# A hybrid attention and state-space decoder layer on Trainium2: score and value matmuls in alternating halves of the array, and the first score behind the middle of the next projection slab

## The chip, the cores and the metric

The kernel runs on one core of a Trainium2 chip. The time is the device time of one execution, in microseconds (us), as a median of runs. One further execution was taken by the hardware profiler; all lines of the profile below are from it. TensorE is PE in the profile (PEld are its weight loads), VectorE is DVE, ScalarE is ACT, GpSimd is POOL, SyncE is SP.

## The reference

One step of a one-layer hybrid decoder: a prompt of 2048 tokens, and 8 sequences with 4 new tokens each (the decode part). One input projection feeds a state-space (Mamba-2) head group and a sliding-window attention head group, then come an output projection, a normalised residual and a feed-forward part. The change lies in the attention of the prompt, which in the reference is

```python
def swa_prompt(q, k, v, sinks):            # window 128: a block and the block before it
    qb = q.astype(jnp.float32).reshape(b, nb, WINDOW, N_KV, Q_PER_KV, HEAD_DIM)   # 16 blocks, 2 x 4 heads of 64
    ...
    s = jnp.einsum('bnqgrd,bnkgd->bngrqk', qb, kk) * (HEAD_DIM ** -0.5)
    s = jnp.where(mask[None, :, None, None], s, -jnp.inf)
    p = sink_softmax(s, sinks.astype(jnp.float32).reshape(N_KV, Q_PER_KV)[:, :, None, None])
    o = jnp.einsum('bngrqk,bnkgd->bnqgrd', p, vv)
    return o.reshape(b, t, ATT_WIDTH).astype(q.dtype)
```

with `q` and `k` turned by a rotary embedding on the first quarter of each head.

## The kernel before

The kernel goes through the tokens in sweeps. Sweep 1 handles the 16 prompt tiles of 128 tokens (and, as one more tile, the decode tokens): it normalises and transposes a tile, projects it to 776 columns (step sizes, q, k, v) and does the attention. Sweep 2 does the state-space part, then follow the output projection and the feed-forward part, which together take most of the time. Tiles are counted from one in this document.

In sweep 1 the work of a tile is cut into steps, and a loop over places calls, at each place, the steps of several tiles: the first slab of 388 columns of tile t (`st_slab(t,0)`), the transposes of the probabilities of tile t-2 (`st_PT`), the scores of tile t-1 (`st_score`), the second slab of tile t, a step of the modulation vector (line 258) or of the decode attention, the values of tile t-2 (`st_PV`), and the transposes of q and k of tile t (`st_qkT`). The calls only set a first order. A scheduler then orders the instructions of TensorE, VectorE, ScalarE and GpSimd by its own model of their times, so that a step's instructions stand among those of others. [...]

To keep precision every operand of the large products is split into a high and a low part, and a product is three matmuls (`mm3`, lines 166 to 168): high with high, high with low, low with high. A slab is 8 x 3 of them, 128 x 128 by 388 columns.

The scores of a tile are 24 matmuls with 64 rows of contraction, by 256 columns (its own block and the one before). The 8 heads lie so that even heads (`par` 0) are in partitions 0 to 63 and odd heads (`par` 1) in partitions 64 to 127, that is, in the lower and the upper half of the array's rows. For each key head g and each `par` six matmuls go into one PSUM bank, and the bank is then copied into `S`, by ScalarE (L434) and by a predicated copy on VectorE (L435), which frees it. After it come the softmax (L384 to L394), and in `st_PT` the transposes (L450) and their copies (`PT` on ScalarE, `PC` on VectorE, L453). The values are four float32 matmuls (L462): two terms, each for g 0 and 1, where g chooses the half of the array's columns. PSUM has three banks for scores and values (`sc`), three for projections (`mm`) and two for transposes (`tr`), each kind used in turn.

Other names: `rt` are the products of the rotary embedding (L374, L375), `qh`, `ql`, `kTh` and `kTl` the split transposes of q and k (L407, L411), `Wx` and `pg` split weights, `xproj` the projection of the convolution's inputs for sweep 2 (`mm<-hT,Wx` and `mm<-hT,pg`), of which the first block's eight run at the end of sweep 1, `dkw` the decays, and `zproj` the first projection of sweep 2 (`mm<-pg,hT`).

Of the kernel before, what the change touches and what calls it, by code (L numbers as in the profile page):

```python
# [119 lines left out]
def body(tc, I, O):  # L120
    nc = tc.nc
    V, S, G, PE, D = nc.vector, nc.scalar, nc.gpsimd, nc.tensor, nc.sync
# [8 lines left out]
    def mm_tile():  # L131
        return ps.tile([128, 512], F32, tag="mm", name="mm", bufs=3)
# [4 lines left out]
    def sc_tile():  # L137
        return ps.tile([128, 512], F32, tag="sc", name="sc", bufs=3)
# [11 lines left out]
    def mm_dec(tmp, w, hs, wt):  # L150
        acc = mm_tile()
        for k in range(8):
            for l in range(2):
                PE.matmul(acc[:2 * ND, :w], lhsT=hs(k), rhs=wt(k, l), start=k + l == 0, stop=k + l == 8)
        S.activation(tmp[:2 * ND, :w], acc[:2 * ND, :w], AF.Copy)
        return tmp

    def sum2(out, tmp, w):
        PE.matmul(out[:ND, :w], lhsT=idt[:2 * ND, 192:224], rhs=tmp[:2 * ND, :w], start=True, stop=True)

    def split(hi, lo, src, eng=None):
        S.activation(hi, src, AF.Copy)  # L162
        (eng or V).tensor_tensor(lo, src, hi.bitcast(F32), ALU.subtract)  # L163

    def mm3(out, ahi, alo, bhi, blo, first=True, last=True):
        PE.matmul(out, lhsT=ahi, rhs=bhi, start=first, stop=False)  # L166
        PE.matmul(out, lhsT=ahi, rhs=blo, start=False, stop=False)  # L167
        PE.matmul(out, lhsT=alo, rhs=bhi, start=False, stop=last)  # L168

    def rstd_of(p, var, P, n=1, scale=1.0):  # L170
        v = p.tile([128, n], F32, tag="ve%d" % n, name="ve", bufs=2)
# [15 lines left out]
    def ptok(t):  # L187
        return 128 if t < NTILE else ND
# [11 lines left out]
    def page(i):  # L200
        return pw.tile([128, 1024], F32R, tag=f"pg{i}", name=f"pg{i}")
# [30 lines left out]
    start = ExitStack()  # L232
# [49 lines left out]
    W1h = [page(k)[:, 0:776] for k in range(8)]  # L282
    W1l = [page(8 + k)[:, 0:776] for k in range(8)]
# [15 lines left out]
    kTh = p1.tile([128, 2, 3, 128], F32R, name="kTh")  # L299
    kTl = p1.tile([128, 2, 3, 128], F32R, name="kTl")  # L300
    tl = {}
# [45 lines left out]
    def st_slab(t, n):  # L347
        P = ptok(t)
        hh = tl["hT", t]
        if n == 0:  # L350
            tl["qkv", t] = p1.tile([128, 648], F32, tag="qkv", name="qkv", bufs=2)
            tl["v", t] = p1.tile([128, 128], F32, tag="v", name="v", bufs=5)
        qkv = tl["qkv", t]
        mm = tl.pop(("sm", t, n)) if t < 3 else mm_tile()
        sl = slice(388 * n, 388 * n + 388)
        if t == NTILE:
            tmp = mm_dec(p1.tile([128, 512], F32, tag="ao", name="tmp", bufs=2), 388, lambda k: hh[:, 0, k, :2 * ND],
                         lambda k, l: (W1l if l else W1h)[k][:, sl])
            sum2(mm, tmp, 388)
        elif t > 2:  # L360
            for k in range(8):
                mm3(mm[:P, :388], hh[:, 0, k, :P], hh[:, 1, k, :P], W1h[k][:, sl], W1l[k][:, sl], k == 0, k == 7)
        if n == 0:
            S.activation(qkv[:P, sl], mm[:P, :388], AF.Copy)
            V.tensor_copy(dt_all[:P, t, :], qkv[:P, 0:8])
            return
        S.activation(qkv[:P, 388:648], mm[:P, 0:260], AF.Copy)
        S.activation(tl["v", t][:P], mm[:P, 260:388], AF.Copy)
        qk = qkv[:P, 8:648].rearrange("p (h d) -> p h d", h=10)
        cos = cc(C_COS + 16 * t, 16)[:P].unsqueeze(1).to_broadcast([P, 10, 16])  # L370
        sin = cc(C_SIN + 16 * t, 16)[:P].unsqueeze(1).to_broadcast([P, 10, 16])
        t1 = p1.tile([128, 10, 16], F32, tag="rt1", name="rt1", bufs=1)
        t2 = p1.tile([128, 10, 16], F32, tag="rt2", name="rt2", bufs=1)
        V.tensor_tensor(t1[:P], qk[:, :, 0:16], cos, ALU.mult)  # L374
        V.tensor_tensor(t2[:P], qk[:, :, 0:16], sin, ALU.mult)  # L375
        V.tensor_tensor(qk[:, :, 0:8], t1[:P, :, 0:8], t2[:P, :, 8:16], ALU.add)
        V.tensor_tensor(qk[:, :, 8:16], t1[:P, :, 8:16], t2[:P, :, 0:8], ALU.add)

    def softmax(p, Sx, P, nh, nk, sink):
        mx = p.tile([128, 8], F32, tag="mx", name="mx", bufs=2)  # L380
        nm = p.tile([128, 8], F32, tag="nm", name="nm", bufs=2)
        su = p.tile([128, 8], F32, tag="su", name="su", bufs=2)
        ex = p.tile([128, 8], F32, tag="ex", name="ex", bufs=2)
        V.tensor_reduce(mx[:P, :nh], Sx, AX.X, ALU.max)  # L384
        V.scalar_tensor_tensor(mx[:P, :nh], mx[:P, :nh], 0.125, sink, ALU.mult, ALU.max)
        V.tensor_scalar(nm[:P, :nh], mx[:P, :nh], -1.0, None, ALU.mult)
        V.tensor_tensor(ex[:P, :nh], sink, mx[:P, :nh], ALU.subtract)
        S.activation(ex[:P, :nh], ex[:P, :nh], AF.Exp)
        for h in range(nh):
            S.activation(Sx[:, h, :], Sx[:, h, :], AF.Exp, bias=nm[:P, h:h + 1], scale=0.125,  # L390
                         accum_out=su[:P, h:h + 1])
        V.tensor_tensor(su[:P, :nh], su[:P, :nh], ex[:P, :nh], ALU.add)
        V.reciprocal(su[:P, :nh], su[:P, :nh])
        G.tensor_tensor(Sx, Sx, su[:P, :nh].unsqueeze(2).to_broadcast([P, nh, nk]), ALU.mult)  # L394
# [20 lines left out]
    def st_score(t):  # L415
        qh, ql = tl.pop(("q", t))
        if t == 0:
            slots, nk, ci = slice(0, 1), 1, 0
        else:
            slots, nk, ci = [(slice(0, 3, 2), 2, 0), (slice(0, 2), 2, 1), (slice(1, 3), 2, 1)][t % 3]  # L420
        ge = cc(C_GE, 128).bitcast(U32).unsqueeze(1).to_broadcast([128, 2, 128])
        Sx = p1.tile([128, 8, 128], F32, tag="S", name="S", bufs=2)
        if t == 0:
            V.memset(Sx, NEG)
        for g in range(2):
            for par in range(2):
                sc = sc_tile().rearrange("p (j s n) -> p j s n", j=2, s=2)
                rp = slice(64 * par, 64 * par + 64)
                for jj in range(2):
                    q2 = 2 * g + jj  # L430
                    mm3(sc[:, jj, 0:nk, :], qh[rp, q2, :], ql[rp, q2, :], kTh[rp, g, slots, :], kTl[rp, g, slots, :])
                hs = slice(4 * g + 2 * par, 4 * g + 2 * par + 2)
                if t > 0:
                    S.activation(Sx[:, hs, :], sc[:, :, 1 - ci, :], AF.Copy)  # L434
                V.copy_predicated(Sx[:, hs, :], ge, sc[:, :, ci, :])  # L435
        softmax(p1, Sx, 128, 8, 128, sm[:, 3, :])
        tl["S", t] = Sx
# [19 lines left out]
    def st_PV(t):  # L457
        terms = tl.pop(("PT", t))
        o = sc_tile()
        for i, (vv, pt) in enumerate(terms):  # L460
            for g in range(2):
                PE.matmul(o[64 * g:64 * g + 64, :], lhsT=vv[:, 64 * g:64 * g + 64], rhs=pt[:, g, :],  # L462
                          start=i == 0, stop=i == len(terms) - 1, tile_position=(0, 64 * g))
        ao = p1.tile([128, 4, 128], F32, tag="ao", name="ao", bufs=2)
        S.activation(ao.rearrange("p r n -> p (r n)"), o, AF.Copy)
        S.dma_start(out=att_d[t], in_=ao)
# [219 lines left out]
    n = len(seq)  # L686
# [66 lines left out]
    for i in range(n + 3):  # L753
        if i == 10:
            start.close()
        g = lambda j: seq[j] if 0 <= j < n else None
# [7 lines left out]
        if t is not None:  # L764
            st_slab(t, 0)
        if g(i - 2) is not None and g(i - 2) < NTILE:
            st_PT(g(i - 2))
        if g(i - 1) is not None and g(i - 1) < NTILE:
            st_score(g(i - 1))
        if t is not None:  # L770
            st_slab(t, 1)
        if i >= 1 and extras:
            extras.pop(0)()
        if g(i - 2) is not None and g(i - 2) < NTILE:
            st_PV(g(i - 2))
# [566 lines left out]
    def dec_steps():  # L1342
# [12 lines left out]
        for n in range(2):  # L1355
            sum2(pp[n], b[:, 512 * n:512 * n + 512], 512)
# [166 lines left out]
```

## Time and profile before

| | |
|---|---|
| median of 3 runs | 2485.43 us (2485.16 to 2487.25) |
| profiled execution, its own time | 2483.86 us |
| its span | 2482.0 us |
| TensorE busy | 2407.5 us, 97% of the span |
| VectorE, ScalarE, GpSimd busy | 1466.3, 764.0, 883.4 us |
| scores of sweep 1, first to last | 66.2 to 391.5 us |

The profile gives for each group of instructions its line, engine, operation, output and inputs by the program's names, shapes, count and busy time. In a timeline a row has start, duration, engine, line, names and the number of records; where an engine sat idle before the row, a bracket gives how long and what ended it. The recorded ends of matmuls are modelled, and successive matmuls overlap in the record. A row of a table by stretches gives for each engine the busy time in the stretch and the number of instructions, then the clock that TensorE was granted (1.00 is full) and the share of the DMA engines.

### The profile page before, as it was taken

Reading aid. Unit: us, or ns where it says so; the run is one execution under the profiler, and the core shown is the slowest. Engines: PE = TensorE matmul, PEld = TensorE weight load, DVE = VectorE, ACT = ScalarE, POOL = GpSimd, SP = SyncE. Lnnn points to the kernel's source line nnn. Section 1 sums busy time; section 2 is a strip of 40 time slices with the busy share of each in tenths; the row PEclk is TensorE's granted clock in tenths of the full one; section 3 lists DMA queues with packets and bytes.
Section 4 is the critical chain, followed back from the end, with each engine's and each line's share of the span. In section 5 each row is a group of like instructions: output and inputs, shape, how many; then the busy total and the mean of one; then the engine's idle time right before and its main releaser. Section 6 shows DMA issues by size and latency. Waiting matters only on the chain.

```text
span 2482.0 us, 32262 instructions
## 1 busy us (share of the span) xinstructions
PE 2407.5 (97%) x12695; PEld 2000.0 (81%) x12695; DVE 1466.3 (59%) x2549; ACT 764.0 (31%) x1546; POOL 883.4 (36%) x587
## 2 busy tenths in 40 slices
PE   7899999999999999899999999999999999999997
PEld 6567777987997888787888888887888888888885
DVE  6756665977788776845444344448744354354347
ACT  3544465432444545221211212112212212212221
POOL 4323430233233222642433424337422332332335
PEclk9999999999999999999999999999999999999998
DMA  8654242223315348221111211119210111111111
GB/s 317 255 186 163 89 157 84 73 67 120 98 62 190 128 161 285 90 66 56 59 43 43 64 43 54 49 37 267 74 52 34 43 60 34 43 60 35 43 47 70
DMA packets 116104, 242.11 MB, mean 98 GB/s; under 512 B 26080, under 2 KB 61360, under 8 KB 112800
## 3 DMA queue, kind: packets, MB, share of 16 engines
q1 hardware_dynamic: 111552, 230.07, 27.6%
q10 hardware_dynamic: 4400, 9.98, 1.0%
q8 instruction: 100, 1.64, 0.3%
q14 instruction: 52, 0.43, 0.1%
HBM read 185.66 MB, written 55.37 MB: 97 GB/s over the span
## 4 chain that ended last, share of the span: by engine, by line
PE 82%; DVE 10%; issue 3%; ACT 2%; POOL 2%; DMA 1%; POOLq 0%; DVEq 0%; SPq 0%; ACTq 0%
PE mm L166 12%; PE mm L168 12%; PE mm L167 12%; PE sc L166 11%; PE sc L167 11%; PE sc L168 11%; PE tr L166 2%; PE tr L168 2%; PE tr L167 2%; PE sc L462 1%; DVE xc L653 1%; PE mm L258 1%; DVE p L1230 1%; DVE csb L858 1%; PE tr L1275 1%
## 5 line engine op out<-in xcount | busy, mean ns | idle before, releaser
L163 POOL TENSOR_TENSOR wdl<-st,wdh 128x1024 fp32r<-128x1024 f32 x63 | 151.6, 2406 | 537.7 <-ACT wdh L162 537.6
L1260 DVE TENSOR_TENSOR r<-r 128x320 f32<-128x320 f32 (+1 forms) x160 | 146.4, 915 | 298.0 <-ACT u L1256 104.7
L1287 DVE TENSOR_TENSOR p<-mm,p 128x512 f32<-128x512 f32 x298 | 202.5, 687 | 175.2 <-PE mm L168 175.2
L162 ACT ACTIVATE wdh<-st 128x1024 fp32r<-128x1024 f32 x63 | 66.8, 1061 | 646.8 <-PE mm L168 263.3
L166 PE MATMUL sc<-H,wvh 128*128 128x352 f32 (+1 forms) x640 | 225.5, 352 | 5.5 <-ACT r L1254 5.5
L167 PE MATMUL sc<-H,wvh 128*128 128x352 f32 (+1 forms) x640 | 225.9, 353 | 0.0
L168 PE MATMUL sc<-H,wvl 128*128 128x352 f32 (+1 forms) x640 | 225.5, 352 | 0.0
L166 PE MATMUL sc<-H,wuh 128*128 128x352 f32 (+1 forms) x640 | 223.8, 350 | 0.0
L168 PE MATMUL sc<-H,wul 128*128 128x352 f32 (+1 forms) x640 | 223.1, 349 | 0.0
L167 PE MATMUL sc<-H,wuh 128*128 128x352 f32 (+1 forms) x640 | 222.8, 348 | 0.0
L1254 ACT ACTIVATE r<-sc 128x352 f32<-128x352 f32 (+1 forms) x160 | 81.5, 510 | 263.9 <-PE sc L168 225.9
L166 PEld LDWEIGHTS sc<-H,wvh 128*128 128x128 f32 x640 | 120.6, 188 | 18.2 <-ACT r L1254 5.9
L167 PEld LDWEIGHTS sc<-H,wvh 128*128 128x128 f32 x640 | 120.6, 188 | 12.3
L168 PEld LDWEIGHTS sc<-H,wvl 128*128 128x128 f32 x640 | 120.5, 188 | 12.1
L166 PEld LDWEIGHTS sc<-H,wuh 128*128 128x128 f32 x640 | 120.1, 188 | 11.1 <-ACT r L1254 0.8
L168 PEld LDWEIGHTS sc<-H,wul 128*128 128x128 f32 x640 | 120.4, 188 | 10.3
L167 PEld LDWEIGHTS sc<-H,wuh 128*128 128x128 f32 x640 | 120.3, 188 | 10.1
L174 POOL TENSOR_TENSOR rs<-ve,mhalf 128x1 f32<-128x1 f32 (+2 forms) x68 | 48.5, 714 | 207.5 <-DVE ve L173 182.7
L1137 DVE TENSOR_TENSOR st<-st,gf 128x1024 f32<-128x1024 f32 x64 | 86.6, 1353 | 50.6 <-POOL wdl L163 42.4
L1259 DVE TENSOR_TENSOR ud<-r 128x32 f32<-128x32 f32 x32 | 58.4, 1825 | 93.8 <-ACT r L1254 93.8
L1287 DVE TENSOR_TENSOR p<-tr,p 128x512 f32<-128x512 f32 x102 | 69.9, 687 | 73.8 <-PE tr L168 73.6
L1261 POOL TENSOR_TENSOR ulx<-r,x 128x512 fp32r<-128x512 f32 (+2 forms) x52 | 76.6, 1475 | 83.5 <-DVE r L1260 83.5
(485 smaller groups left out, 6608.9 us busy)
## 6 DMA issues: line engine op xcount, KB each, us to landing
st<-in_wd SPq DMA_DIRECT2D x64, 512.0 KB
st<-in_wu SPq DMA_DIRECT2D x63, 512.0 KB
wa<-in_w_ada SPq DMA_DIRECT2D x32, 512.0 KB
hT_d<-hb SPq DMA_DIRECT2D x16, 1024.0 KB
hT<-hT_d SPq DMA_DIRECT2D x16, 512.0 KB
hT<-hT_d SPq DMA_DIRECT2D x8, 1024.0 KB
csb<-cs_d SPq DMA_DIRECT2D x16, 512.0 KB
p<-xhat_d SPq DMA_DIRECT2D x16, 512.0 KB
```

Source lines behind the costliest of these rows:

```text
L162: S.activation(hi, src, AF.Copy)
L163: (eng or V).tensor_tensor(lo, src, hi.bitcast(F32), ALU.subtract)
L166: PE.matmul(out, lhsT=ahi, rhs=bhi, start=first, stop=False)
L167: PE.matmul(out, lhsT=ahi, rhs=blo, start=False, stop=False)
L168: PE.matmul(out, lhsT=alo, rhs=bhi, start=False, stop=last)
L174: G.tensor_tensor(r[:P], v[:P], mhalf[:P, 0:n], ALU.pow)
L1137: V.tensor_tensor(st, raw, scale, ALU.mult)
L1254: S.activation(r[:, :n], mm[:, :n], AF.Relu)
L1259: V.tensor_tensor(ud, r[:, w:n], r[:, w:n], ALU.mult)
L1260: V.tensor_tensor(r[:, :w], r[:, :w], r[:, :w], ALU.mult)
L1261: G.tensor_tensor(ul[:, o:o + w], r[:, :w], uh[:, o:o + w].bitcast(F32), ALU.subtract)
L1287: V.tensor_tensor(acc[t][:, sl], mm, acc[t][:, sl], ALU.add)
```

## The change

A helper `side_by_side` issues a list of matmuls and gives each an ordering after the one before it in the list. The ordering is one for the scheduler (`NoSync`): it fixes their order in TensorE's row and adds no semaphore. The scores of a key head use it with the two halves in turn (`par` 1, 0, 1, 0 ...) and both banks taken ahead of them; for g = 1 the second half's bank is now one of the projection banks. The first score of a tile is ordered behind the twelfth of the 24 matmuls of the next tile's first slab (`tl["mid"]`, from the fourth tile on). The four value matmuls get the same helper, with g 1, 0, 1, 0.

```diff
+    def side_by_side(calls, prev=None):
+        for fn in calls:
+            ins = fn()
+            if prev is not None:
+                tc.add_manual_dep(ins.ins, prev.ins.name,
+                                  mybir.DependencyInfo(mybir.DependencyClass.NoSync, mybir.DependencyReason.DATA),
+                                  reason="side_by_side")
+            prev = ins
...
     def st_slab(t, n):
...
-                mm3(mm[:P, :388], hh[:, 0, k, :P], hh[:, 1, k, :P], W1h[k][:, sl], W1l[k][:, sl], k == 0, k == 7)
+                ins = mm3(mm[:P, :388], hh[:, 0, k, :P], hh[:, 1, k, :P], W1h[k][:, sl], W1l[k][:, sl], k == 0, k == 7)
+                if n == 0 and k == 3:
+                    tl["mid"] = ins
...
     def st_score(t):
...
+        mid = tl.pop("mid", None)
+        rp = lambda par: slice(64 * par, 64 * par + 64)
         for g in range(2):
+            scs = [(sc_tile, mm_tile)[g * par]().rearrange("p (j s n) -> p j s n", j=2, s=2) for par in range(2)]
+            side_by_side([lambda jj=jj, i=i, par=par: PE.matmul(
+                scs[par][:, jj, 0:nk, :], lhsT=(ql if i == 2 else qh)[rp(par), 2 * g + jj, :],
+                rhs=(kTl if i == 1 else kTh)[rp(par), g, slots, :], start=i == 0, stop=i == 2)
+                for jj in range(2) for i in range(3) for par in (1, 0)], mid)
             for par in range(2):
-                sc = sc_tile().rearrange("p (j s n) -> p j s n", j=2, s=2)
-                rp = slice(64 * par, 64 * par + 64)
-                for jj in range(2):
-                    q2 = 2 * g + jj
-                    mm3(sc[:, jj, 0:nk, :], qh[rp, q2, :], ql[rp, q2, :], kTh[rp, g, slots, :], kTl[rp, g, slots, :])
+                sc = scs[par]
...
     def st_PV(t):
...
-        for i, (vv, pt) in enumerate(terms):
-            for g in range(2):
-                PE.matmul(o[64 * g:64 * g + 64, :], lhsT=vv[:, 64 * g:64 * g + 64], rhs=pt[:, g, :],
-                          start=i == 0, stop=i == len(terms) - 1, tile_position=(0, 64 * g))
+        side_by_side([lambda i=i, vv=vv, pt=pt, g=g: PE.matmul(
+            o[64 * g:64 * g + 64, :], lhsT=vv[:, 64 * g:64 * g + 64], rhs=pt[:, g, :], start=i == 0,
+            stop=i == len(terms) - 1, tile_position=(0, 64 * g))
+            for i, (vv, pt) in enumerate(terms) for g in (1, 0)])
```

The lines of the new kernel are numbered a little higher: the three matmuls of a slab are L175 to L177, the scores L440, their copies L448 and L449, the transposes of the probabilities L464, the values L474, those of q and k L418 and L422, the rotary products L385 and L386.

TensorE's row in the scores of one middle tile, before (the tile of the timeline at 138 to 148 us in the prediction): six matmuls of one half stand far behind the others.

```order
L168 MATMUL sc<-kTh,ql 128x256
L166 MATMUL sc<-kTh,qh 128x256
L167 MATMUL sc<-kTl,qh 128x256
L168 MATMUL sc<-kTh,ql 128x256
L168 MATMUL mm<-pg_128,hb_101 128x388
L258 MATMUL mm<-wa,scT 32x512 x5
L450 MATMUL tr<-idt,S 128x128 x4
L258 MATMUL mm<-wa,scT 32x512
L450 MATMUL tr<-idt,S 128x128 x4
L258 MATMUL mm<-wa,scT 32x512 x2
L166 MATMUL sc<-kTh,qh 128x256
L167 MATMUL sc<-kTl,qh 128x256
```

The same in the new kernel: four matmuls of the first key head, some slab matmuls and transposes, and then the other 20 close together, those of the last half of the second key head into a projection bank.

```order
L330 MATMUL tr<-idt,x 128x128 x4
L440 MATMUL sc<-kTl,qh 128x256 x2
L440 MATMUL sc<-kTh,ql 128x256 x2
L440 MATMUL sc<-kTh,qh 128x256 x2
L440 MATMUL sc<-kTl,qh 128x256 x2
L440 MATMUL sc<-kTh,ql 128x256 x2
L440 MATMUL mm<-kTl,qh 128x256
L440 MATMUL sc<-kTl,qh 128x256
L440 MATMUL mm<-kTh,ql 128x256
L464 MATMUL tr<-idt,S 128x128 x4
L440 MATMUL sc<-kTh,ql 128x256
L440 MATMUL mm<-kTh,qh 128x256
```

The six of the last half now alternate with six others. Of the value matmuls, the old row has one pair torn apart by other work in 8 of the 16 tiles (the x2 of one line broken into two rows with others between), the new row in none.

VectorE's row around two weight splits, `Wx`, before: the four copies of a tile's scores (L435) stand behind the two rotary products,

```order
L163 TENSOR_TENSOR Wx_3688<-wb_102,Wx_3687 128x1024
L163 TENSOR_TENSOR Wx_3866<-hbuf,Wx_3865 128x1024
L374 TENSOR_TENSOR rt_3484<-qkv,c_137 128x160
L375 TENSOR_TENSOR rt_3485<-qkv,c_137 128x160
L435 COPY_PREDICATED S<-c_137,sc 128x256 x3
L453 TENSOR_TENSOR PC<-tr,cst 128x512
L376 TENSOR_TENSOR qkv<-rt_3484,rt_3485 128x10x8
L377 TENSOR_TENSOR qkv<-rt_3484,rt_3485 128x10x8
L453 TENSOR_TENSOR PC<-tr,cst 128x512
L435 COPY_PREDICATED S<-c_137,sc 128x256
```

and in the new kernel, where all four stand ahead of them:

```order
L172 TENSOR_TENSOR Wx_3866<-hbuf,Wx_3865 128x1024
L449 COPY_PREDICATED S<-c_137,sc 128x256 x2
L449 COPY_PREDICATED S<-c_137,mm 128x256
L449 COPY_PREDICATED S<-c_137,sc 128x256
L385 TENSOR_TENSOR rt_3302<-qkv,c_137 128x160
L386 TENSOR_TENSOR rt_3303<-qkv,c_137 128x160
L395 TENSOR_REDUCE mx<-S 128x8
```

The end of sweep 1 on TensorE, before: the last tile's transposes of q and k stand among the projections of the convolution's inputs (`mm<-hT,...`), most of which come before them; the tile's scores follow later.

```order
L407 MATMUL tr<-idt,qkv 128x128 x2
L462 MATMUL sc<-PT,v 64x512
L462 MATMUL sc<-PC,vd 64x512
L407 MATMUL tr<-idt,qkv 128x128 x2
L167 MATMUL mm<-hT_3856,Wx_3865 128x256
L168 MATMUL mm<-hT_3855,Wx_3866 128x256
L166 MATMUL mm<-hT_3855,pg_3981 128x256
L462 MATMUL sc<-PC,vd 64x512
L411 MATMUL tr<-idt,kd 128x128 x2
L167 MATMUL mm<-hT_3856,pg_3981 128x256
L168 MATMUL mm<-hT_3855,pg_3982 128x256
L166 MATMUL mm<-hT_3855,pg_3985 128x256
```

In the new kernel the last tile's transposes and first scores come before the first of those projections.

```order
L177 MATMUL mm<-pg_128,hb_104 128x388
L474 MATMUL sc<-PT,v 64x512 x2
L474 MATMUL sc<-PC,vd 64x512 x2
L418 MATMUL tr<-idt,qkv 128x128 x4
L422 MATMUL tr<-idt,kd 128x128 x2
L440 MATMUL sc<-kTh,qh 128x256 x2
L440 MATMUL mm<-kTh,qh 128x256
L440 MATMUL sc<-kTh,qh 128x256
L175 MATMUL mm<-hT_3855,Wx_3683 128x256
L176 MATMUL mm<-hT_3856,Wx_3683 128x256
```

In ScalarE's row the tables of activation functions are loaded ten times in the stretch from the last slabs to the end of sweep 1 before, and three times in the new kernel. From the first projections of sweep 2 on the rows of the engines are the same in both.

More of the change, by code (lines that the diff above doesn't have):

```diff
@@ L167, in mm3 @@
         PE.matmul(out, lhsT=ahi, rhs=blo, start=False, stop=False)
-        PE.matmul(out, lhsT=alo, rhs=bhi, start=False, stop=last)
+        return PE.matmul(out, lhsT=alo, rhs=bhi, start=False, stop=last)
     def rstd_of(p, var, P, n=1, scale=1.0):
```

## The prediction

> **What bounds the kernel now.** I read the page's busy shares and its chain first, then busy time by stretches of the first sweep, where the change lies, and last the instructions of the score and value lines in time.
>
> ```profile
> PE 2407.5 (97%) x12695; PEld 2000.0 (81%) x12695; DVE 1466.3 (59%) x2549; ACT 764.0 (31%) x1546; POOL 883.4 (36%) x587
> PE 82%; DVE 10%; issue 3%; ACT 2%; POOL 2%; DMA 1%; POOLq 0%; DVEq 0%; SPq 0%; ACTq 0%
> ```
>
> TensorE is busy 97% of the span and carries 82% of the chain that ended last. That is a mean; the stretches say where a TensorE microsecond is worth a microsecond.
>
> ```profile
> core 0: us, PE busy (x) PEld busy (x) DVE busy (x) ACT busy (x) POOL busy (x), PEclk, DMA share, GB/s
> 60.00:85.00 25.00, 18.11 (x110) 9.88 (x108) 22.62 (x56) 14.53 (x42) 15.71 (x14) 0.80 0.98 384
> 85.00:305.00 220.00, 220.00 (x1287) 160.25 (x1286) 135.09 (x353) 103.02 (x331) 71.18 (x61) 1.00 0.44 149
> 306.00:312.10 6.10, 0.00 (x0) 0.00 (x0) 6.10 (x6) 1.72 (x4) 6.10 (x4) 0.90 1.02 302
> 312.10:318.00 5.90, 5.89 (x16) 3.08 (x16) 3.93 (x9) 0.38 (x1) 0.74 (x1) 0.52 0.99 366
> 320.00:345.00 25.00, 25.00 (x147) 21.17 (x147) 12.56 (x34) 16.60 (x54) 10.03 (x7) 1.00 0.24 85
> 345.00:400.00 55.00, 49.09 (x338) 38.43 (x336) 45.25 (x117) 43.04 (x113) 13.29 (x8) 0.94 0.26 89
> ```
>
> From 85 to 305 us TensorE is never without work (220.00 of 220.00) at full clock, and again from 320 to 345; VectorE is busy 61% of the first stretch, ScalarE 47%. There every slot taken out of TensorE's row shortens the kernel, until another engine is late. At 306 there is a hole of 6 us with 5.9 us at half clock (0.52) behind it. In the tail, 345 to 400 us, VectorE (45.25) and ScalarE (43.04) are nearly as full as TensorE (49.09), so slots saved there are worth little.
>
> Now the matmuls that the change reorders. Their recorded durations overlap, so what a matmul costs is read from one start to the next. These are the scores of one tile (those of the other middle tiles read alike), in TensorE's order of time:
>
> ```profile
> 138.40 0.34 PE L166 MATMUL mm<-pg,hb 128*128 128x388 f32 x1
> 138.58 0.34 PE L167 MATMUL mm<-pg,hb 128*128 128x388 f32 x1
> 138.85 0.50 PE L166 MATMUL sc<-kTh,qh 64*128 64x256 f32 x3
> 139.28 1.09 PE L321 MATMUL tr<-idt,x 128*128 128x128 f32 x8
> 140.30 0.39 PE L167 MATMUL sc<-kTl,qh 64*128 64x256 f32 x1
> 140.53 0.28 PE L168 MATMUL sc<-kTh,ql 64*128 64x256 f32 x1
> 140.53 0.38 PE L167 MATMUL sc<-kTl,qh 64*128 64x256 f32 x1
> ...
> 141.69 0.44 PE L168 MATMUL mm<-pg,hb 128*128 128x388 f32 x1
> ...
> 147.02 0.38 PE L166 MATMUL sc<-kTh,qh 64*128 64x256 f32 x1
> ...
> 147.60 0.28 PE L167 MATMUL sc<-kTl,qh 64*128 64x256 f32 x1
> 147.72 0.28 PE L168 MATMUL sc<-kTh,ql 64*128 64x256 f32 x1
> 147.92 1.08 PE L462 MATMUL sc<-PT,v 128*64 128x512 f32 x4
> ```
>
> Three things are to be seen. A score matmul of one half follows another of the same half after 0.12 us (147.60, 147.72). Two of different halves start in the same instant (140.53 twice). And the second happens already before the change: the 15 matmuls from 140.30 take 1.39 us, not 15 x 0.12 = 1.8; TensorE reaches ahead across the five or so rows between two halves. A run's ends cost too: its first start comes 0.27 after the slab's (138.58 to 138.85) where two slab matmuls are 0.18 apart (138.40, 138.58), and the first slab matmul behind a run of halves takes 0.28 (130.54 to 130.82, further below). I count these two tenths, 0.19, for every run, and what lies between as the run's own.
>
> **The change, part by part.** *Scores.* In the tile above the three runs take 139.28 - 138.85 = 0.43, 141.69 - 140.30 = 1.39 and 147.92 - 147.02 = 0.90, together 2.72 us. The last six stand alone because they are all of one half, and their bank, the fourth, comes free late from the pool of three. In the changed row a tile is 4 + 20 matmuls with halves in turn, 2 and 10 slots: by the 0.12 just read and 0.2 for a run's first matmul and its way out (the 0.90 of six slots is 0.2 + 6 x 0.117), 0.43 and 1.37, 1.80 us. That is 0.92 less, and one run fewer, 0.19: 1.1 us a tile. Thirteen tiles (the third to the fifteenth; the first is small, the second lies in the start, the last in the tail) give 14. Read in the same way tile by tile the old ones take 2.5 to 3.4 us in two to four runs, the new ones 1.8 to 2.1 in two or three: the same 14 in sum, one tile as little as 0.6.
>
> *Values.* In TensorE's order of time:
>
> ```profile
> 129.53 1.08 PE L462 MATMUL sc<-PT,v 128*64 128x512 f32 x4
> 130.54 0.44 PE L166 MATMUL mm<-pg,hb 128*128 128x388 f32 x1
> 130.82 0.34 PE L167 MATMUL mm<-pg,hb 128*128 128x388 f32 x1
> ...
> 131.45 1.07 PE L462 MATMUL sc<-PC,vd 128*64 128x512 f32 x2
> 132.45 0.44 PE L407 MATMUL tr<-idt,qkv 128*128 128x128 f32 x2
> 132.82 1.07 PE L462 MATMUL sc<-PC,vd 128*64 128x512 f32 x2
> ```
>
> A float32 matmul leaves two records, so x4 is two matmuls, one in each half, and x2 is one alone. Two side by side take 130.54 - 129.53 = 1.01 us; one alone takes 1.00. A lone value matmul therefore wastes its whole 1.0 us. In the old row 8 of 16 tiles have one pair torn so; in the new one every pair stands together. 8 x (1.0 + 0.19) = 9.5, of which one lies in the tail: 9 taken.
>
> *The hole at 306.* The rows are VectorE's, the last TensorE's:
>
> ```profile
> 304.24 1.80 DVE L163 TENSOR_TENSOR Wx<-wb,Wx 128x1024 fp32r<-128x1024 f32 x1
> 305.96 2.07 DVE L163 TENSOR_TENSOR Wx<-hbuf,Wx 128x1024 fp32r<-128x1024 f32 x1
> 307.95 2.46 DVE L374 TENSOR_TENSOR rt<-qkv,c 128x160 f32<-128x160 f32 x1
> 310.33 1.38 DVE L375 TENSOR_TENSOR rt<-qkv,c 128x160 f32<-128x160 f32 x1
> 311.63 1.10 DVE L435 COPY_PREDICATED S<-c,sc 128x256 f32<-128x256 uint32 x3
> 312.11 0.58 PE L166 MATMUL sc<-kTh,qh 64*128 64x256 f32 x1 [6.12 <-DVE S L435]
> ```
>
> The fourth group of scores needs a score bank; the copy that frees one stands on VectorE behind two weight splits and two rotary products, 7.7 us. In the new row the fourth group takes a projection bank, and all four copies stand ahead of the rotary products. TensorE then has slabs, scores and values before it needs the rotated keys. The hole (6.1) goes and so does most of the half clock behind it: 5.9 us at 0.52 lose 2.8. I take 8 of these 8.9 and leave 1 for what is late next, the transposes of q that wait for the rotary products. The bank borrowed from the projections (three of them) delays a slab only if both its copies come later than the two other banks last, 24 slab matmuls of 0.18 each, 4.3 us a bank; outside this hole no copy is that late. Cost nothing, at most the hole again.
>
> *New waits.* NoSync orderings add no semaphore, but hold a row in place: at three of the late tiles (13 to 15) the transposes of q and k are followed at once by the first scores, where they had slabs between. The scores then wait for the ScalarE split of q and k and whatever stands behind. First pieces of the chain (start, length), then rows of TensorE and VectorE in time:
>
> ```profile
> 361.51 1.28 ACT L681
> 365.67 2.70 ACT S L390 x14
> 382.84 0.49 ACT qh L162
> ```
> ```profile
> 346.68 3.38 DVE L163 TENSOR_TENSOR pg<-xb,pg 128x1024 fp32r<-128x1024 f32 x1
> 391.08 0.38 PE L166 MATMUL sc<-kTh,qh 64*128 64x256 f32 x1 [1.96 <-DVE S L435]
> 397.73 0.80 PE L569 MATMUL mm<-dkw,cst 128*128 128x128 f32 x2 [2.87 <-DVE dkw L560]
> 400.20 0.80 PE L166 MATMUL mm<-pg,hT 128*128 128x512 f32 x1
> ```
>
> About 1 us each (two splits of 0.49): 4 with the third tile's, which has one slab matmul for cover. Bounds 1 to 8.
>
> *The start.* The second tile's scores now precede the fourth tile's first slab, while 60 to 85 us has 6.9 us of idle TensorE that DMA and VectorE set (DMA share 0.98, VectorE 22.62 of 25). Nearest rows: the idle can shrink by a few us or the slab can come later by a tile's score run, 2.7. Taken 0, bounds -2 to +3.
>
> *The tail.* In the old row the eight convolution-input projections stand among the last three tiles' scores and fill TensorE while the last tile's rotation and splits run. In the new row the first four scores of the sixteenth tile stand ahead of all eight, behind the transposes of a q that is not yet rotated. So TensorE must wait there. Price: rotary products of 2.46 + 1.38 with splits of up to 3.38 (346.68) on VectorE ahead, less some 2 us of values and slabs in front, and then a softmax run of 14 exponentials (2.70) with a table load (1.28) ahead of the split of q on ScalarE: 7 to 9 us, and at most 12. An idle of that length slows the clock, as at 306: another 2.8. Against this, the two stalls of 1.96 and 2.87 shown, and the run overheads of two tiles' scores, were in the old tail, and ScalarE has 7 fewer table loads there (10 in the old row, 3 in the new, 1.28 each), which shortens the alternation of exponentials and silu. The scores of tiles 14 and 15 are done before the tail instead of in it, already counted. Net +5 taken, bounds -6 to +15.
>
> The clock can be weighed. The row shows 0.52 for 5.9 us after 6.1 idle. [...]
>
> *Sum.* -14 - 9 - 8 + 4 + 0 + 5 = -22. The profiled execution took 2483.86, 1.57 under the median of 2485.43; 2461.9 by its own time, 2463.5 as a median. From sweep 2's projections on, rows are the same.
>
> **Rivals.** About 5 us, 0.2%, is what a measurement here can tell from no change.
>
> *A: the tail eats it.* If the first scores of the last tile wait for a VectorE that still has all its splits and copies queued (45.25 us of work in the 55), each us of wait counts in full, since the eight projections (8 x 24 matmuls of 0.12, 22 us of TensorE) stand behind it. It decides at a net tail cost of 27 us in place of 5; 12 of wait and 2.8 of clock is what rows give, and starting VectorE's queue with two splits adds 6. For slower it would need 32: 2490. Chance 0.09.
>
> *B: halves in turn don't pair for long.* The rows show pairs where TensorE's reach let two halves meet, never 20 matmuls in strict turn, each with a weight load of its own; loads already fill 160 of the 220 us. If every second pair slips by a slot, scores give half, 7, and the sum is -15: 2470. Against it: the meeting half of the 15 ran in 10 slots without a slip. Chance 0.12.
>
> *C: the hole stays.* If the rotated keys are needed at once, the splits and rotary products (7.7) stop TensorE at the transposes instead: -22 + 8 = -14: 2471. For it: VectorE's row there is the same but for the copies' place. Chance 0.13.
>
> B and C, or either with a bad tail (+15): -4, no change to be seen: 2481. Chance 0.10.
>
> *D: the tail gains.* With fewer table loads and two tiles' softmax out of it, the tail ends 6 earlier than before in place of 5 later: 2452. Chance 0.13.
>
> **How the numbers follow.** The forecast, 2463.5 within 2457 to 2469, has 0.43. It and B, C and D are all faster: 0.43 + 0.12 + 0.13 + 0.13 = 0.81. Same 0.10, slower 0.09. The range reaches at the low end to D with all of the values' and scores' terms, the start at its -2 and the whole hole (2449), at the high end to the middle of the unchanged cases (2483, a bad tail of +15 with waits of 8, a start of +3 and a slip in the scores); the slower cases, some unchanged ones and a still larger gain stay outside, 0.2 together.
>
> **What would show it.** Between the start and the first decode step TensorE stays full, and a tile's score slots fall from 2.7 to 1.8 us in two runs; value matmuls always show x4 in about 1.0 us or x8 in 1.9. The row of 6.12 before the score line vanishes, and 310 to 318 runs at clock 1.00. The first matmul of sweep 2's z projection, 400.20 now, starts about 378. Wrong would be: score runs that still take 2.5 us a tile with halves in turn; a new idle row of over 15 us at the last tile's first scores with the projections behind it; or a slab that waits for a projection bank held by score copies.

## The result, and the profile after

The changed kernel takes 2468.53 us (median of 4 runs, 2464.62 to 2470.42) against 2485.42 before: 0.9928 of it, 95% interval 0.9911 to 0.9946, 16.9 us faster. The profiled execution took 2467.27 us, its span is 2465.4. Busy shares and chain of the page after:

```profile
PE 2378.6 (96%) x12695; PEld 1987.0 (81%) x12695; DVE 1454.9 (59%) x2549; ACT 748.8 (30%) x1536; POOL 886.9 (36%) x587
PE 75%; DVE 10%; issue 2%; ACT 2%; POOL 1%; DMA 1%; POOLq 0%; DVEq 0%; ACTq 0%; SPq 0%
```

TensorE is busy 28.9 us less, but the span fell by only 16.6. Busy time by stretches, after, shows where the rest went:

```profile
core 0: us, PE busy (x) PEld busy (x) DVE busy (x) ACT busy (x) POOL busy (x), PEclk, DMA share, GB/s
85.00:305.00 220.00, 208.98 (x1330) 155.25 (x1323) 142.27 (x369) 109.34 (x360) 83.22 (x67) 0.99 0.49 170
305.00:345.00 40.00, 37.00 (x244) 29.29 (x242) 24.16 (x54) 24.58 (x76) 13.17 (x7) 1.00 0.29 94
345.00:390.00 45.00, 36.73 (x267) 31.78 (x268) 32.06 (x95) 23.20 (x72) 9.73 (x6) 0.89 0.35 119
```

From 85 to 305 us, where TensorE had been full before, it now stands still for 11 us. The hole behind 306 is gone, and 305 to 345 runs at clock 1.00; just ahead of it, behind a new wait at 300.78, TensorE worked 3.4 us at 0.50 (301.6 to 305, rows further below).

The scores and values of one middle tile after, TensorE's rows in time:

```profile
115.20 0.38 PE L440 MATMUL sc<-kTh,qh 64*128 64x256 f32 x2
115.43 0.28 PE L440 MATMUL mm<-kTh,qh 64*128 64x256 f32 x1
115.43 0.28 PE L440 MATMUL sc<-kTh,qh 64*128 64x256 f32 x1
115.64 0.45 PE L175 MATMUL mm<-pg,hb 128*128 128x388 f32 x1
...
119.55 0.39 PE L440 MATMUL sc<-kTl,qh 64*128 64x256 f32 x2
...
120.73 0.28 PE L440 MATMUL mm<-kTh,ql 64*128 64x256 f32 x1
120.94 0.45 PE L176 MATMUL mm<-pg,hb 128*128 128x388 f32 x1
...
125.29 1.08 PE L474 MATMUL sc<-PT,v 128*64 128x512 f32 x4
126.20 1.03 PE L474 MATMUL sc<-PC,vd 128*64 128x512 f32 x4
127.16 0.66 PE L418 MATMUL tr<-idt,qkv 128*128 128x128 f32 x4
```

Four scores take 0.44 us (115.20 to 115.64) and the other 20 take 1.39 (119.55 to 120.94): 1.83 a tile, where 1.80 was forecast. All four value matmuls take 1.87 together (125.29 to 127.16).

For the comparison I gave the time from each matmul's start to the next one's to the kind of the first (its slot), and counted idle gaps of over 0.2 us apart, from 60 us to the start of the fourth slab of sweep 2's z projection (456.7 before, 439.7 after; behind it the two traces differ by under 0.2 us until 870 us). All sums are worked out from the starts in the traces, in us; "median" and the ratio are of the whole kernel:

| kernel | scores | values | other | idle | sum | median | ratio, interval |
|---|---|---|---|---|---|---|---|
| before | 46.2 | 40.0 | 290.3 | 19.9 | 396.4 | 2485.4 | |
| after | 31.2 | 30.3 | 286.6 | 31.4 | 379.5 | 2468.5 | 0.9928 (0.9911 to 0.9946) |
| e1, values ordered | 48.0 | 32.0 | 289.7 | 19.6 | 389.3 | 2475.4 | 0.9962 (0.9950 to 0.9975) |
| e2, scores changed | 30.5 | 38.4 | 289.2 | 31.1 | 389.2 | 2475.2 | 0.9958 (0.9943 to 0.9973) |
| e4, no projection bank | 36.5 | 33.1 | 288.8 | 26.6 | 385.0 | 2473.2 | 0.9953 (0.9938 to 0.9968) |
| e5, bank only | 37.2 | 39.4 | 286.7 | 24.8 | 388.1 | 2473.7 | 0.9951 (0.9936 to 0.9966) |
| e7, bank and values | 36.2 | 29.9 | 284.6 | 27.1 | 377.8 | 2467.0 | 0.9928 (0.9913 to 0.9943) |
| e8, blocks of six | 40.6 | 29.9 | 285.3 | 27.4 | 383.2 | 2469.2 | 0.9937 (0.9922 to 0.9952) |
| e6c, cover in the tail | 30.8 | 30.3 | 286.5 | 27.1 | 374.7 | 2462.8 | 0.9913 (0.9898 to 0.9927) |
| e6b, cover | 32.0 | 31.5 | 283.2 | 20.8 | 367.5 | 2452.6 | 0.9873 (0.9857 to 0.9889) |
| e9, cover, free order | 36.3 | 32.0 | 282.1 | 19.0 | 369.4 | 2456.7 | 0.9884 (0.9867 to 0.9900) |
| e10, cover alone | 44.4 | 42.0 | 290.3 | 18.7 | 395.4 | 2481.0 | 0.9985 (0.9975 to 0.9994) |

The change: -15.0 scores, -9.7 values, -3.7 other work, and +11.5 idle: -16.9. Of the other work 3.5 is the modulation's matmuls (line 258), which use a quarter of the array's columns each (128*32 in the rows). A step has 8 of them, two records each. Rows of TensorE, one step before:

```profile
120.45 1.91 PE L258 MATMUL mm<-wa,scT 128*32 128x512 f32 x12
...
123.18 1.05 PE L258 MATMUL mm<-wa,scT 128*32 128x512 f32 x4
```

and after:

```profile
123.44 1.92 PE L267 MATMUL mm<-wa,scT 128*32 128x512 f32 x16
```

Torn in two they take 1.84 + 0.98 = 2.82 from first start to the next work's, together 1.85. The old row has the eight steps in 16 pieces, the new one in 10, a side effect of the new order that the prediction doesn't have.

Idle rows of TensorE after, the longest and those of the late tiles, with what ended them:

```profile
76.93 1.94 PE L330 MATMUL tr<-idt,xb 128*128 128x128 f32 x8 [5.50 <-DVE mv L190]
106.95 1.08 PE L474 MATMUL sc<-PT,v 128*64 128x512 f32 x4 [1.30 <-ACT PT L465]
166.31 1.03 PE L272 MATMUL mm<-part,idt 128*9 128x512 f32 x2 [2.18 <-ACT part L270]
300.78 0.39 PE L440 MATMUL sc<-kTh,qh 64*128 64x256 f32 x2 [3.61 <-ACT kTh L171]
319.07 0.39 PE L440 MATMUL sc<-kTh,qh 64*128 64x256 f32 x2 [0.74 <-ACT kTh L171]
334.21 0.39 PE L440 MATMUL sc<-kTh,qh 64*128 64x256 f32 x2 [0.80 <-ACT kTh L171]
346.13 1.11 PE L418 MATMUL tr<-idt,qkv 128*128 128x128 f32 x4 [2.49 <-DVE qkv L388]
351.61 0.58 PE L440 MATMUL sc<-kTh,qh 64*128 64x256 f32 x2 [3.93 <-ACT kTh L171]
364.04 1.08 PE L474 MATMUL sc<-PT,v 128*64 128x512 f32 x4 [2.30 <-DVE S L449]
```

Six of these nine waits end with ScalarE, three with VectorE. What ScalarE did before 300.78, its rows after:

```profile
295.84 0.40 ACT L401 ACTIVATE S<-S,nm 128x128 f32<-128x128 f32 x1 [3.39 <-DVE nm L397]
...
298.64 0.39 ACT L401 ACTIVATE S<-S,nm 128x128 f32<-128x128 f32 x1
...
299.03 0.47 ACT L375 ACTIVATE qkv<-mm 128x388 f32<-128x388 f32 x1
299.40 0.58 ACT L171 ACTIVATE qh<-tr 128x512 fp32r<-128x512 f32 x1
299.88 0.58 ACT L479 ACTIVATE ao<-sc 128x512 f32<-128x512 f32 x1
300.35 0.37 ACT L171 ACTIVATE kTh<-tr 128x256 fp32r<-128x256 f32 x1
...
347.00 0.63 ACT L171 ACTIVATE pg<-wzst 128x512 fp32r<-128x512 f32 x1 [1.99 <-DMA wzst<-in_wz]
```

The transposes of q and k are done at 297.2; their splits stand in ScalarE's row behind the softmax of the tile before (295.84 to 299.03) and two other copies. The scores stand right behind the transposes on TensorE, with the slabs behind them. At the last tile the same comes on top of a weight split that waited 1.99 for its DMA (347.00).

### The profile page after: what moved, and what is told of

The parts are those of the page before. It is cut to its first block, busy times and chain, and to the rows that moved or that the text cites. A ratio compares the mean times of both kernels' runs of the same rounds, so it can differ in the third digit from the quotient of the medians.

```text
span 2465.4 us, 32261 instructions
## 1 busy us (share of the span) xinstructions
PE 2378.6 (96%) x12695; PEld 1987.0 (81%) x12695; DVE 1454.9 (59%) x2549; ACT 748.8 (30%) x1536; POOL 886.9 (36%) x587
## 4 chain that ended last, share of the span: by engine, by line
PE 75%; DVE 10%; issue 2%; ACT 2%; POOL 1%; DMA 1%; POOLq 0%; DVEq 0%; ACTq 0%; SPq 0%
PE mm L175 11%; PE mm L177 11%; PE mm L176 11%; PE sc L175 11%; PE sc L176 11%; PE sc L177 11%; PE tr L175 2%; PE tr L177 2%; PE tr L176 2%; DVE xc L667 1%; DVE p L1244 1%; PE tr L1289 1%; DVE p L1301 1%; PE sc L932 1%; PE sc L1129 1%
## 5 line engine op out<-in xcount | busy, mean ns | idle before, releaser
L175 PE MATMUL sc<-H,wvh 128*128 128x352 f32 (+1 forms) x640 | 225.6, 353 | 5.6 <-ACT r L1268 5.6
L177 PE MATMUL sc<-H,wvl 128*128 128x352 f32 (+1 forms) x640 | 225.5, 352 | 0.0
L175 PE MATMUL sc<-H,wuh 128*128 128x352 f32 (+1 forms) x640 | 223.8, 350 | 0.0
L177 PE MATMUL sc<-H,wul 128*128 128x352 f32 (+1 forms) x640 | 223.1, 349 | 0.0
L175 PEld LDWEIGHTS sc<-H,wvh 128*128 128x128 f32 x640 | 120.6, 188 | 18.3 <-ACT r L1268 6.0
L176 PEld LDWEIGHTS sc<-H,wvh 128*128 128x128 f32 x640 | 120.6, 189 | 12.3
L177 PEld LDWEIGHTS sc<-H,wvl 128*128 128x128 f32 x640 | 120.6, 189 | 12.1
L175 PEld LDWEIGHTS sc<-H,wuh 128*128 128x128 f32 x640 | 120.1, 188 | 11.1 <-ACT r L1268 0.8
L177 PEld LDWEIGHTS sc<-H,wul 128*128 128x128 f32 x640 | 120.4, 188 | 10.2
L176 PEld LDWEIGHTS sc<-H,wuh 128*128 128x128 f32 x640 | 120.3, 188 | 10.1
```

What stands on the lines that cost most here:

```text
L177: return PE.matmul(out, lhsT=alo, rhs=bhi, start=False, stop=last)
```

## The experiments

**e1, e2: each half of the change.** e1 keeps the old `st_score`, e2 the old `st_PV`.

```diff
# e1: the change, with st_score of the kernel before
# e2: the change, with st_PV of the kernel before
```

> Only the value matmuls are ordered, the scores stay as before. Theory (slots saved on TensorE by pairing, each kind separately): value slots fall by about 8 to 9 us, score slots by 1 to 2 (the row falls a little otherwise), the 6 us hole at the weight splits stays because the fourth score group still needs a score bank: -9 to -12, about 2475. Rival (the values' slots are covered by waits elsewhere, the whole gain is the scores' and the bank's): within 4 us of before, 2482 to 2487.

> Only the scores are changed (halves in turn, fourth group in a projection bank), the values stay as before. Theory: score slots -14 to -16, the hole at the weight splits (-6 and its half clock) goes, new waits of scores right behind the transposes of k come in (+8 to +14): 2472 to 2478. Rival (values are worth nothing): the same as the whole change, 2468.

Measured -8.9 and -9.1 us against the same runs of before; together 18.0, and the whole change 16.9: the two halves add up. e1: values -8.0, as expected, idle unchanged; its rival falls. Two things came otherwise than I had written: score slots rose by 1.8 instead of falling, and the hole at the weight splits did not stay, though e1 has neither the fourth bank nor the new order of scores. Its VectorE row is another one, with the copy of the scores behind the splits and ahead of the next rotary products, which start at 320.38:

```profile
305.94 2.80 DVE L172 TENSOR_TENSOR Wx<-hbuf,Wx 128x1024 fp32r<-128x1024 f32 x1
...
309.27 0.44 DVE L446 COPY_PREDICATED S<-c,sc 128x256 f32<-128x256 uint32 x1
```

e2: scores -15.7, idle +11.2, nearly all of the change's idle time. So the waits come in with the scores' new order and bank, not with the values.

**e5, e4: the bank alone, and the order without the bank.**

```diff
# e5, in the kernel before
-                sc = sc_tile().rearrange("p (j s n) -> p j s n", j=2, s=2)
+                sc = (sc_tile, mm_tile)[g * par]().rearrange("p (j s n) -> p j s n", j=2, s=2)
# e4, in the changed kernel
-            scs = [(sc_tile, mm_tile)[g * par]().rearrange("p (j s n) -> p j s n", j=2, s=2) for par in range(2)]
+            scs = [sc_tile().rearrange("p (j s n) -> p j s n", j=2, s=2) for par in range(2)]
```

> Only the bank: the fourth score group takes a projection bank, no matmul is ordered by hand. Theory A (TensorE's reach across the two halves pairs them by itself once the last six need not stand apart): score slots -10 to -12, that is two thirds or more of the whole change's score gain, hole gone, fewer new waits: 2468 to 2473. Rival B (the alternating order makes the pairs): score slots fall by less than 5, only the hole goes: 2477 to 2481.

> The whole change but for the bank: the fourth score group takes the pool of three score banks again, matmuls in alternating order as in the change. Theory A (the bank closes the hole and lets the last twelve stand together): value slots -8 to -10, score slots -9 to -11, but a stall of 5 to 7 us at the weight splits comes back: 2472 to 2479. Rival B (the alternating order is enough): as the whole change, 2466 to 2470.

e5: -10.6 us, and score slots -9.0 of the change's -15.0 with no matmul ordered by hand. The time lies at the upper end of theory A's, above 2473 by 0.7; the slots are 1.0 short of A's 10 to 12, but far from B's (under 5). e4: values -6.9 (8 to 10 expected), scores -9.7, and the stall is there, in TensorE's row:

```profile
302.17 0.58 PE L440 MATMUL sc<-kTh,qh 64*128 64x256 f32 x1 [6.78 <-DVE S L449]
```

That is the old hole, 6.78 for 6.12, with the same releaser. The alternating order alone doesn't close it; in the change it is the fourth bank that does, as the prediction said. It is not the only way: in e1 another order of VectorE's row closed it without the bank. For the slots the two parts overlap: the bank alone takes 9.0, the order alone 9.7, both together 15.0.

**e7, e8: the order of the halves.** e7 has the bank and the ordered values, with the scores as the scheduler puts them; e8 chains six and six.

```diff
# e7: the change, with st_score as in e5
# e8, in the changed kernel
-                for jj in range(2) for i in range(3) for par in (1, 0)], mid)
+                for par in (1, 0) for jj in range(2) for i in range(3)], mid)
```

> Bank and ordered values, but the scores' matmuls in the scheduler's own order. Theory (the parts add up as slots, less new waits): score slots -8 to -10 by the bank alone, values -9, idle time +3 to +7: 2469 to 2473, 1 to 4 above the whole change. Rival (the alternating order itself is worth its 6 us of slots in full): 2474 to 2477.

> The whole change, but the twelve scores of a key head are chained with six of one half and then six of the other. Theory A (TensorE reaches past at least six rows to the other half, so six and six also run side by side): a run of 22 takes 1.4 to 1.9 us, score slots 4 to 7 above those of the change, 2472 to 2477. Rival B (only neighbours pair): a run of 22 takes 2.4 to 2.8 us, score slots 15 or more above, 2483 or more.

First and last rows of a run of 20 in e7, which stand as blocks of five of one half and five of the other, with the slab's matmul behind:

```profile
117.45 0.38 PE L176 MATMUL sc<-kTl,qh 64*128 64x256 f32 x1
...
118.86 0.28 PE L177 MATMUL mm<-kTh,ql 64*128 64x256 f32 x1
119.07 0.44 PE L177 MATMUL mm<-pg,hb 128*128 128x388 f32 x1
```

A run of 22 in e8, five or six of one half at a time:

```profile
120.46 0.38 PE L440 MATMUL sc<-kTl,qh 64*128 64x256 f32 x1
...
121.16 0.28 PE L440 MATMUL mm<-kTl,qh 64*128 64x256 f32 x1
121.27 0.28 PE L440 MATMUL sc<-kTl,qh 64*128 64x256 f32 x1
121.29 0.28 PE L440 MATMUL mm<-kTh,ql 64*128 64x256 f32 x1
121.39 0.28 PE L440 MATMUL sc<-kTh,ql 64*128 64x256 f32 x1
...
122.31 0.45 PE L176 MATMUL mm<-pg,hb 128*128 128x388 f32 x1
```

The 20 take 1.39 in strict turn, 1.62 in blocks of five (117.45 to 119.07) and 1.85 for 22 in blocks of six (120.46 to 122.31), where 22 one behind another would be 0.2 + 22 x 0.117 = 2.8 (an estimate, by the row of six at 147.02 in the prediction). Six and six therefore run mostly side by side: e8's theory A holds for the run (1.4 to 1.9), its rival falls; its score slots are 9.4 above the change's, more than the 4 to 7 of A, and its time, 2469.2, is still below the 2472 that I expected. e7 takes 2467.0 with 5.0 us more score slots than the change. Both are the change's time within their intervals: idle time fell by 4.3 and 4.0 as slots rose. In a row that has to wait for ScalarE anyway, arriving a little later at the wait costs little; for e8 that covers under half of the 9.4, and its sum is 3.7 above the change's, which the medians can't tell apart. So e7's theory holds for the slots (-10.1), and its time is lower than both theories had it.

**e6b, e6c: cover for the late tiles.** If the waits for `kTh` are what was lost, work between the transposes of k and the first score should bring it back. In e6b this is done from the loop's place 12 on, in e6c for the last tile only; in both the loads of four weights (`w2_load`) move ahead with the first projections.

```diff
+    def behind(ins, prev):                 # an ordering for the scheduler, as side_by_side
...
     def st_slab(t, n):
...
+                if late() and n == 1 and k == 1 and "kdT" in tl:
+                    behind(ins, tl.pop("kdT"))          # last transpose of k of the tile before
+                if n == late() and k == (7 if late() else 3):
                     tl["mid"] = ins
...
+        if t is not None and late():
+            st_slab(t, 1)
+        if t is None and i == n:
+            xproj(0, range(2))              # its first slab behind kdT, its second is the last tile's "mid"
         if g(i - 1) is not None and g(i - 1) < NTILE:
             st_score(g(i - 1))
-        if t is not None:
+        if t is not None and not late():
             st_slab(t, 1)
```

> The whole change, and cover for the late tiles: from the 11th place on the transposes of k are chained ahead of the next tile's second slab and the first score behind its end; the last tile's first score behind two of the eight projections of the convolution's inputs. Theory (what was lost against the sum of slots are scores that stand right behind the transposes of k and wait for ScalarE's split behind a softmax): the waits of 3.6, 0.7, 0.8 and 3.9 us for kTh vanish, idle falls by 6 to 10: 2459 to 2463. Rival (the wait moves to the transposes, which then wait for the rotary products, or to ScalarE's other work): 2466 to 2472.

> As the kernel before this one, but with cover for the last tile alone. Theory: only the waits of the tail (3.9 for kTh, part of 2.5 and 2.3) vanish, 2462 to 2465. Rival (the tail is bound by ScalarE and VectorE, so a wait taken from TensorE there comes back): 2467 to 2470.

e6b takes 2452.6, 32.7 below before and some 16 below the change, more than the theory's 2459 to 2463. Stretches of e6b:

```profile
305.00:345.00 40.00, 38.84 (x271) 31.18 (x269) 27.51 (x55) 28.73 (x84) 18.85 (x12) 1.00 0.38 127
345.00:379.00 34.00, 30.61 (x222) 24.21 (x221) 28.97 (x97) 22.95 (x72) 4.05 (x3) 0.95 0.22 80
```

and the late tile's transposes and the last tile's first score, with no idle time ahead of them:

```profile
313.50 0.44 PE L433 MATMUL tr<-idt,kd 128*128 128x128 f32 x2
313.69 0.42 PE L181 MATMUL mm<-pg,hb 128*128 128x388 f32 x1
...
345.24 0.39 PE L451 MATMUL sc<-kTh,qh 64*128 64x256 f32 x2
```

Idle fell by 10.6 to 20.8, 5.1 of it in the tail, where the clock now shows 0.95 for 0.89, and the sum by 12.0. The profiled spans differ by 14.4 (2465.4 and 2451.0); 1.8 of the rest comes near 1000 us, where the same work stood at clock 0.50 for 10.2 us in the one and 6.8 in the other, and can't be credited to the cover. The z projection, still 390.45 after the change, starts at 378.7. The waits did not move to the transposes, except for 1.60 at 296 and 0.55 and 0.61 at the last tile. e6c takes 2462.8, as its theory had it: 5.8 below the change by the medians, though the intervals of the two ratios overlap. In the traces idle in the tail fell by 5.6 and the sum by 4.8. So most of what is taken from TensorE's waits there is kept, and the rival, that VectorE and ScalarE bind the tail, gets no support.

**e9, e10: is the cover a gain of its own?** e9 is e6b with scores as in e5, their first matmuls behind the cover; e10 is the kernel before with the cover alone.

```diff
# e9, e10: e6b, with the old loop of st_score, in it
+                    behind(PE.matmul(o_, lhsT=qh[rp, q2, :], rhs=kh_, start=True, stop=False), mid)
# e9: the bank of e5 and the ordered values; e10: three score banks and the old values
```

> Cover for the late tiles, the bank and the ordered values, but scores in the scheduler's own order behind their first matmuls. Theory (once TensorE has no idle time that the slots can hide in, the order in turn is worth its slots): score slots 3 to 6 above the covered change, 2455 to 2459. Rival (the order in turn is worth nothing): 2451 to 2454.

> The kernel before with the cover for the late tiles alone: no projection bank, scores and values in their old order. Theory (the cover removes waits that the change made; before it there was only the hole at the weight splits, which the cover doesn't touch): 2479 to 2487. Rival (the cover is a gain of its own, independent of the change): 2470 to 2475, about as much below before as the covered change lies below the change.

e10: -3.4 us (0.9975 to 0.9994), within theory: there was little to cover before. Most of the cover's 16 us were the change's own loss. e9: 2456.7, scores 4.3 above e6b; in the middle of the theory's span, but its interval (0.9867 to 0.9900) overlaps with e6b's (0.9857 to 0.9889), so whether the order in turn is worth its 4 us once the waits are gone is not settled.

No run was made without the ordering behind the middle of the slab: leaving it out gives the same rows on all engines, so that part of the change does nothing here.

## Why the prediction was right or wrong, point by point

The time, 2468.5, lies in the range and 5 above the forecast; the sign was right. To compare term by term, the half rate has to be counted by itself: while the granted clock is 0.50, I count half of the time that TensorE works as lost, an estimate by that clock (after, projection matmuls start 0.21 apart at 353 us, at clock 0.50, and 0.12 apart at 360, at 1.00). These are all such stretches of the part compared, before:

```profile
68.60:78.80 10.20, 5.67 (x21) 3.42 (x20) 9.56 (x27) 5.03 (x19) 5.75 (x7) 0.50 1.01 405
310.90:317.80 6.90, 5.69 (x15) 3.08 (x16) 5.13 (x11) 0.38 (x1) 1.94 (x2) 0.51 1.01 369
392.90:403.10 10.20, 7.33 (x23) 4.42 (x20) 7.13 (x26) 6.30 (x26) 1.61 (x1) 0.50 0.07 27
```

and after:

```profile
66.10:69.50 3.40, 3.40 (x22) 1.07 (x16) 2.71 (x5) 0.66 (x3) 2.62 (x2) 0.50 1.01 416
76.30:86.50 10.20, 8.08 (x36) 4.11 (x37) 7.24 (x20) 3.87 (x15) 7.47 (x7) 0.50 0.66 256
301.60:305.00 3.40, 3.40 (x14) 3.31 (x13) 0.69 (x1) 0.34 (x1) 1.05 (x1) 0.50 0.12 46
346.00:356.20 10.20, 6.13 (x28) 5.51 (x29) 5.79 (x13) 8.19 (x27) 6.00 (x4) 0.50 0.45 151
```

With half of the work in them moved from scores, values and other work to the start, the hole and the tail (an estimate, by the starts in the traces within these stretches), the terms are, in us:

| term | forecast | measured |
|---|---|---|
| scores | -14 | -14.2 |
| values | -9 | -7.5 |
| hole, with its half rate | -8 | -7.2 |
| new waits | +4 | +12.3 |
| start, with its half rate | 0 | +5.6 |
| tail, with its half rate | +5 | +2.0 |
| modulation's matmuls | not in the sum | -5.8 |
| other work | not in the sum | -2.1 |
| together | -22 | -16.9 |

So that the time came within 5 of the forecast is in part luck: waits and start cost 14 more than taken, and over half of that came back from modulation matmuls and other work, which the sum put at nothing, and from a tail that cost less.

- *Scores, -14, and values, -9*: -15.0 and -9.7 in slots, by the mechanism given; e1 and e2 show each alone. Some 2.2 of the 9.7 is not pairing: 4.5 us of the old value matmuls stood in the half-rate stretches behind the hole and in the tail. The run ends that the prediction counted with the two lie in the other work. What was wrong in the reasoning is what makes the pairs. I gave them to the forced order; e5 and e7 show that 9 to 10 of the 15 come with the fourth bank and no forced order, which lets the last six stand beside the others, where they pair (20 in 1.62 in e7). e4 shows as much, 9.7, for the order without the bank. The rival "halves in turn don't pair for long" fell: 20 in strict turn take 10 slots.
- *The hole, -8*: gone, and e4 brings it back by taking the bank away (e1 loses it without the bank). Of its half clock only part went, since behind the wait at 300.78 (3.61) there is now a shorter stretch at 0.50, 3.4 us from 301.6. The rival that it stays fell.
- *New waits, +4, bounds 1 to 8*: this is the step that failed. Between the start and the tail (90 to 345 us), idle is 12.3, all of it new (the 6.1 before were the hole). I priced the wait for the splits of q and k at about 1 us a tile, two splits of 0.49 (the third tile's, 1.00 at 81.90, is counted in the start). At two of the three late tiles it was 0.74 and 0.80; at the other, 3.61, a whole softmax stood ahead on ScalarE (3.2 us from 295.84 to 299.03), which I counted for the last tile only. The larger part, 7.1, lies where I had priced nothing: 1.30 and 2.18 with a softmax ahead of the copies for values and for the modulation, 1.25 and 0.68 in the decode attention, and several of about 0.4. TensorE probably meets them because, with fewer score slots, it arrives earlier; no run shows that by itself.
- *The start, 0*: idle rose by 2.7 (6.8 to 9.5), near the upper bound, and TensorE worked 11.5 us at half rate for 5.7 before, which loses another 2.9: in all 5.6, outside the bounds.
- *The tail, +5*: the wait was there, 2.49 + 3.93 = 6.4 for 7 to 9; idle rose by 2.6 (7.0 to 9.6), and e6c takes 5.6 of it away. The half clock that I added to its price is no new cost, since the old tail had as much, 7.3 us of work at 0.50 from 392.9 to 403.1 for 6.1 after the change. Behind the wait itself, from 351.6 to 356.2, 4.6 us at 0.50 lose 2.3 by the same count, where 2.8 was taken from the hole. With +2.0 in all, the rivals A (the tail eats the gain, 27) and D (it gains, -6) fell.
- *What would show it*: the z projection's start, forecast at 378, came at 390.45. The last tile's transposes of probabilities and values, which had stood behind that start (406.96 to 415.02 before), now stand ahead of it; 7 of the 17 us appear only behind it. The place was badly chosen, and the end isn't touched by it. TensorE did not stay full ahead of the first decode step either (1.30 and 2.18). None of the signs of being wrong came.

## What to carry to other kernels

Before forcing the order of small matmuls that use halves of the array, see whether they merely stand apart for want of a bank: here one more bank alone took 9 of the 15 us of score slots, TensorE paired the halves itself (20 in 1.62 us in e7), and with bank and ordered values the forced order of scores changed the time by nothing that these runs can tell (2467.0 and 2468.5); with the waits covered, 4 us are open (e9). When slots are taken out of a full engine, price the next wait by the whole queue that stands ahead of its releaser, a softmax included (3.2 us of it ahead of the wait of 3.61 at 300.78), and check each place where the producer is directly followed by its consumer. Putting a slab's worth of independent work between them gained nearly as much again as the whole change (e6b, 32.7 us below before).

## What the runs showed of the hardware

In e8's trace the recorded starts of TensorE do not follow its row strictly. The five matmuls into the projection bank (`mm`, the upper half) stand behind six of the lower half in the row, but the first of them started at 121.16, ahead of the last two of those six, at 121.27 and 121.39. The 22 of that run took 1.85 us, where one behind another would be 2.8 by the estimate above; that fits the early starts (the ends are modelled). How far such a reach goes was not measured.
